# Encoder layer on one core: eight U blocks loaded during the query projection, four more at the start of the seam, seven gathers moved from the seam to the stage before it, and the loop's gathers spread by a table

## The chip, the cores and the metric

The kernel runs on one core of one Trainium2 chip. The metric is the device time of one execution in microseconds. Three runs of the kernel before took 1572.16, 1577.76 and 1579.21 us; the median, 1577.76 us, is what the new time is compared with.

## The reference

One transformer layer on 512 tokens of width 1024, all in float32. Two attentions and a projection come first; they matter here only as what runs before. The part that the change touches is the mixture of 16384 experts ("PEER") behind them:

```
q   = h @ w_q                          # 8 heads x 256, two halves of 128
s1, s2 = q1 @ keys0, q2 @ keys1        # 128 scores each; top 16 of each
idx = e1 * 128 + e2                    # top 16 of the 16x16 sums: 128 experts per token
hpre = sum_d x[t,d] * u_table[idx[t,e], d]
act  = softmax_weight * gelu(hpre)
out  = sum_e act[t,e] * v_table[idx[t,e], :]
h    = layer_norm(alpha*h + out + sigmoid(h @ gate_w + b) * (p @ ple_w))
```

U and V have 16384 rows of 1024 numbers (64 MB each).

## The kernel before, in words

The 512 tokens are four chunks of 128, and the experts of a token are found in one of two ways.

**Chunk 0 by gathers.** For each of its 128 slots k, GpSimd issues an indirect DMA that brings for all 128 tokens the row `u[idx[:,k]]` (128 rows of 4 KB, 0.524 MB), and VectorE multiplies it with h and sums it (`gather_u`, L1148; `rows`, L888). After all 128 and a Gelu, 128 more gathers bring V rows, and VectorE adds each, scaled, to the output (`gather_v`, L1157). That is 257 steps in all (128 U, one Gelu, 128 V).

**Chunk 1** has its U part done by gathers too (`own_rows`, 128 of them), its V part densely. **Chunks 2 and 3 (256 tokens, `N_U`) densely:** every block of 128 U rows (0.524 MB) is multiplied with the tokens on TensorE, and a Gelu follows. One-hot products turn the selected weights into a dense matrix G, which is stored in DRAM (`g_dram`); in the main loop G times the Gelu is split in a high and a low part and multiplied with the V block of 128 experts (three products for float32 accuracy).

In order of time:

1. **Query projection**, 16 groups (loop at L700): SP loads a slice of `w_q` (0.524 MB) into a `raw` buffer (three of them), ScalarE and VectorE cut it in two parts, TensorE multiplies. Then VectorE finds the top 16.
2. **Lead stage** (L1067 to L1097), written out by hand on all engines. TensorE works through 105 (`LEAD`) U blocks (`lead_block`, L935) that are mixed with the gate projection and the one-hot products; how many lie between two VectorE steps is set by a running account (`run_pe`, L812). `lead_block` keeps three loaded or loading blocks ahead in the `raw` buffers (`load_u`, L915). VectorE does the routing (`route`), the one-hot matrices (`build_g`, L821), and the products of the gathered rows. These come in the buffers `whi`, `wlo` and `row`, two of each. With the last `build_g`, chunk 0's first 24 (`BESIDE`) gathers run; then come the closing `pb.close()` and the next stage.
3. **The seam** (L1191 to L1210), also by hand: seven gathers are issued by GpSimd into `gat` buffers (eight, `GATS`), then GpSimd's two loads of the first G tile (`g_near`); the rest of the U blocks, the first three V blocks, and gathers up to step 42 (`PRE`), so that 18 gathers stand in the seam.
4. **Main loop** (L1214), 128 V blocks: in the first 23 passes (n from 0 to 22) one more U block is also loaded and multiplied by `expert_in` (L637) in three products. SP loads the V block and, from n = 28, a stored Gelu `ge`. G tiles are loaded some passes ahead (`g_loads`). In each pass some of the remaining 215 gather steps are run: the counter `spent` grows by 1 for n from 1 to 22, then by a half (`LATE`), and the steps done follow it. VectorE and SP run in the written order; a gather's product on VectorE stands behind the pass's own split.
5. Four layer norms and stores.

Each engine runs its instructions in order, so a wait holds all that is queued behind it. SP's DMAs are issued in order as well.

Of the kernel before, what the change touches and what calls it, by code (L numbers as in the profile page):

```python
# [9 lines left out]
F32 = mybir.dt.float32  # L10
# [26 lines left out]
WIDE = 40  # L37
LEAD = 105
# [4 lines left out]
LAG = 6.0  # L43
PRE = 42
BESIDE = 24
OWN = 1.2
OWN_G = 0.65
OWN_LATE = 10.0
LATE = 0.5
OT = 8  # L50
# [5 lines left out]
GATS = 8  # L56
NO_GATHER = 1
# [12 lines left out]
def tile_encoder_layer(ctx: ExitStack, tc: tile.TileContext, A: dict, out: bass.AP):  # L70
    nc = tc.nc
# [613 lines left out]
    def sub_scores(g, ps):  # L685
# [38 lines left out]
    pb = ExitStack()  # L724
    bt = pb.enter_context(tc.tile_pool(name="bt", bufs=2, side="right", reuse_waits="tile"))
    rg = pR.enter_context(tc.tile_pool(name="rg", bufs=1, reuse_waits="tile"))
# [183 lines left out]
    raws = []  # L910
# [3 lines left out]

    def load_u():  # L915
        nonlocal loaded
        if loaded < LEAD:
            raw = wst.tile([128, 8, 128], F32, name="raw", bufs=3)
            raws.append((loaded, raw))
            ins = nc.sync.dma_start(raw, A["uT"][loaded])  # L920
            if not loaded:
                tc.keep_in_program_order(ins)
            loaded += 1
# [11 lines left out]
    def lead_block():  # L935


        while len(raws) < 3 and loaded < LEAD:
            load_u()
        if not raws:  # L940
            return
        i, raw = raws.pop(0)
        ps = psH.tile([128, 512], F32, name="hp") if gating else ps_tile("mm", 4)
        for k in range(8):
            nc.tensor.matmul(ps[:, :N_U], raw[:, k], whole[:, k, :], start=(k == 0), stop=(k == 7))  # L945
            if k == 3 and last:
                leave_u(*last.pop())
            if k % 2 and tasks:
                tasks.pop(0)()
            yield PRODUCT_U  # L950
        last.append((i, ps))
# [115 lines left out]
    with tc.manual_schedule(engines={nc.vector.engine, nc.scalar.engine, nc.tensor.engine, nc.sync.engine,  # L1067
                                     nc.gpsimd.engine}):
        for _ in range(3):
            load_u()  # L1070
# [120 lines left out]
    with tc.manual_schedule(engines={nc.vector.engine, nc.scalar.engine, nc.tensor.engine, nc.sync.engine,  # L1191
                                     nc.gpsimd.engine}):
        gating = True
        some = [fetch_u(0, BESIDE + k) for k in range(GATS - 1)]
        for lo, hi in ((128 // GT, NTG), (0, 128 // GT)):
            load_g(0, lo, hi, nc.gpsimd)
        blocks_ahead(2)
        v_next = [load_v(n) for n in range(2)]
        for u in range(7):
            gather_u(0, BESIDE + u, some[u])  # L1200
# [3 lines left out]
        for n in range(2):  # L1204
            v_cut[n] = cut_v(n)
            blocks_ahead(1)
        for k in range(BESIDE + 7, PRE):
            gather_u(0, k)
        for _ in pe_work:
            pass  # L1210
    done, spent = PRE, 0
    with tc.manual_schedule(engines={nc.vector.engine, nc.sync.engine}):
        expert_in(LEAD)
        for n, i in enumerate(order):  # L1214
# [44 lines left out]
            for x in g_loads.get(n, []):  # L1259
                load_g(*x)  # L1260
            if n >= NO_GATHER:
                spent += 1 if n + LEAD < 128 else LATE
            upto = min(len(steps), PRE + math.ceil((len(steps) - PRE) * spent / (128 - (1 - LATE) * LEAD - 3 - NO_GATHER)))
            for f in steps[done:upto]:
# [107 lines left out]
```

## Time and profile before

| | before |
|---|---|
| median of three runs | 1577.76 us |
| profiled execution, its own time | 1580.15 us |
| its span, first to last instruction | 1578.2 us |
| mean granted TensorE clock | 0.988 |
| TensorE matmul busy | 1505.8 us (95%) |
| VectorE busy | 1298.2 us (82%) |
| DMA moved | 460.40 MB, mean 292 GB/s |

Times in the profile count from the span's start. A row of a timeline gives start, duration, engine, line, instruction, number merged, and in brackets how long the engine had been idle and what ended that. In a table of windows the columns are the busy time of each engine in that stretch (number of instructions in brackets), then the granted TensorE clock (1.00 is full speed), the mean busy share of the 16 DMA engines, and what they moved. A single matmul's record is longer than its place in the row of matmuls, since they are pipelined, so rows that merge many are used for durations.

### The profile page before, as it was taken

The numbers are of one execution on the slowest core, as the hardware profiler recorded it, in microseconds if no ns is written. First come the engines' busy times: TensorE is split into PE (matmuls) and PEld (weight loads), VectorE is DVE, ScalarE is ACT, GpSimd is POOL, SyncE is SP. The second block draws the span as 40 slices with busy tenths as digits, with TensorE's granted clock in tenths as the row PEclk, the third lists the DMA queues.
The fourth block names the chain that finished last, engine by engine and source line by source line (L and its number), as shares of the span: only waits on it lengthen the run. The fifth ranks groups of instructions, "written<-read, shape, count | busy, mean of one in ns | idle before, by whom it ended". The sixth has DMA issues, their size and how long they took to land.

```text
span 1578.2 us, 22819 instructions
## 1 busy us (share of the span) xinstructions
PE 1505.8 (95%) x7707; PEld 1267.9 (80%) x7707; DVE 1298.2 (82%) x3022; ACT 657.3 (42%) x1234; POOL 565.8 (36%) x521
## 2 busy tenths in 40 slices
PE   6999999999998999999999978999799999999997
PEld 4788777788887889789889967888588888788885
DVE  7376685679889799898889738998699899898997
ACT  3365675333222566167425512443233333333333
POOL 1023100020014334443323146555445666565630
PEclk9999999999999999999999999999999999999998
DMA  7242241142379899999989799999999999999972
GB/s 230 64 116 88 79 121 41 55 149 81 99 235 349 306 392 392 409 416 417 417 321 410 283 390 393 390 399 392 338 393 370 398 386 399 395 392 398 387 300 80
DMA packets 202532, 460.40 MB, mean 292 GB/s; under 512 B 17968, under 2 KB 104368, under 8 KB 199344
## 3 DMA queue, kind: packets, MB, share of 16 engines
q1 hardware_dynamic: 127888, 213.55, 38.1%
q0 software_dynamic: 58400, 208.69, 34.5%
q10 hardware_dynamic: 16128, 36.71, 6.0%
q8 instruction: 61, 1.00, 0.3%
q14 instruction: 55, 0.45, 0.1%
HBM read 415.11 MB, written 40.89 MB: 289 GB/s over the span
## 4 chain that ended last, share of the span: by engine, by line
PE 62%; DMA 19%; DVE 13%; issue 3%; ACT 2%; SPq 1%; POOL 0%; ACTq 0%; POOLq 0%; DVEq 0%
PE mm L945 7%; PE acc L108 6%; PE acc L109 6%; PE acc L110 6%; PE hp L945 6%; DMA raw<-in_v_rows_dram 6%; PE mm L108 4%; PE mm L110 4%; DMA v_raw<-in_v_rows_dram 4%; PE mm L109 4%; PE tr L841 4%; PE pj L108 3%; PE pj L109 3%; DMA raw<-in_uT_dram 3%; PE pj L110 3%
## 5 line engine op out<-in xcount | busy, mean ns | idle before, releaser
L1159 POOL DMA_INDIRECT gat<-in_v_rows_dram,i_sel x128 | 217.3, 1697 | 138.8 <-DVE base L1161 115.6
L945 PE MATMUL mm<-whole,raw 128*128 128x256 f32 x1088 | 244.0, 380 | 3.3 <-DMA raw<-in_uT_dram 3.0
L945 PEld LDWEIGHTS mm<-whole,raw 128*128 128x128 f32 x1088 | 202.5, 190 | 32.7 <-ACT ge L927 3.9
L108 PE MATMUL acc<-v_hi,a_hi 128*128 128x512 f32 x456 | 180.1, 397 | 15.8 <-ACT a_hi L93 15.6
L93 ACT CAST whi<-raw 128x1024 fp32r<-128x1024 f32 (+4 forms) x118 | 118.4, 1003 | 182.7 <-DMA raw<-in_v_rows_dram 60.4
L1144 POOL DMA_INDIRECT gat<-in_u_rows_dram,i_sel x104 | 136.0, 1308 | 147.9 <-DVE gat L1150 89.9
L110 PE MATMUL acc<-v_hi,a_lo 128*128 128x512 f32 x456 | 179.9, 396 | 0.1
L109 PE MATMUL acc<-v_lo,a_hi 128*128 128x512 f32 x456 | 179.3, 395 | 0.2 <-DVE v_lo L94 0.2
L94 DVE TENSOR_TENSOR wlo<-raw,whi 128x1024 fp32r<-128x1024 f32 (+4 forms) x118 | 136.7, 1159 | 40.8 <-ACT whi L93 39.9
L1161 DVE SCALAR_TENSOR_TENSOR base<-gat,hdot,base 128x1024 f32<-128x1024 f32 x128 | 163.8, 1280 | 1.5
L945 PE MATMUL hp<-whole,raw 128*128 128x256 f32 x592 | 137.1, 389 | 11.5 <-DMA raw<-in_uT_dram 11.0
L1150 DVE SCALAR_TENSOR_TENSOR gat<-gat,h 128x1024 f32<-128x1024 f32 x104 | 122.8, 1218 | 28.3 <-DMA gat<-in_u_rows_dram,i_sel 28.3
L93 ACT CAST v_hi<-v_raw 128x1024 fp32r<-128x1024 f32 x76 | 79.9, 1051 | 146.2 <-DMA v_raw<-in_v_rows_dram 123.3
L945 PEld LDWEIGHTS hp<-whole,raw 128*128 128x128 f32 x592 | 114.7, 195 | 29.6 <-issue 12.2
L892 POOL DMA_INDIRECT whi<-in_u_rows_dram,s_ix x43 | 45.9, 1069 | 208.3 <-DVE cand L745 132.5
L108 PE MATMUL acc<-whi,a_hi 128*128 128x512 f32 x300 | 117.2, 391 | 2.8 <-ACT a_hi L93 2.8
L110 PE MATMUL acc<-whi,a_lo 128*128 128x512 f32 x300 | 117.4, 391 | 0.0
L109 PE MATMUL acc<-wlo,a_hi 128*128 128x512 f32 x300 | 117.0, 390 | 0.0
L875 DVE TENSOR_SCALAR oh_j<-iota,eT 128x128 f32<-128x128 f32 x384 | 116.3, 375 | 0.0
L108 PEld LDWEIGHTS acc<-v_hi,a_hi 128*128 128x128 f32 x456 | 86.6, 191 | 36.1 <-ACT a_hi L93 18.9
L110 PEld LDWEIGHTS acc<-v_hi,a_lo 128*128 128x128 f32 x456 | 86.9, 190 | 21.1 <-DVE a_lo L94 2.9
L109 PEld LDWEIGHTS acc<-v_lo,a_hi 128*128 128x128 f32 x456 | 87.0, 191 | 18.6 <-DVE v_lo L94 0.9
(367 smaller groups left out, 3326.4 us busy)
## 6 DMA issues: line engine op xcount, KB each, us to landing
raw<-in_uT_dram SPq DMA_DIRECT2D x128, 512.0 KB
v_raw<-in_v_rows_dram SPq DMA_DIRECT2D x78, 512.0 KB
raw<-in_v_rows_dram SPq DMA_DIRECT2D x50, 512.0 KB
g_dram<-g_st ACTq DMA_DIRECT2D x24, 1024.0 KB
ge_dram<-ge ACTq DMA_DIRECT2D x88, 128.0 KB
ge<-ge_dram SPq DMA_DIRECT2D x88, 128.0 KB
g_wide<-g_dram SPq DMA_DIRECT2D x9, 1024.0 KB
raw<-in_w_in_dram SPq DMA_DIRECT2D x17, 512.0 KB
```

Of the source, the lines that this page charges most:

```text
L93: nc.scalar.copy(hi, src)
L94: nc.vector.tensor_tensor(lo, src, r32(hi), op=OP.subtract)
L108: nc.tensor.matmul(ps, a[0], b[0], start=start, stop=False)
L109: nc.tensor.matmul(ps, a[0], b[1], start=False, stop=False)
L110: nc.tensor.matmul(ps, a[1], b[0], start=False, stop=stop)
L841: nc.tensor.matmul(ps[:, i * 128:(i + 1) * 128], oj[:, 4 * r + i, :], oi[:, 4 * r + i, :], start=True, stop=True)
L875: nc.vector.tensor_scalar(oj[:, i], iota, eT[:, 1, t0 + i:t0 + i + 1], eT[:, 2, t0 + i:t0 + i + 1], op0=OP.is_equal, op1=OP.mult)
L945: nc.tensor.matmul(ps[:, :N_U], raw[:, k], whole[:, k, :], start=(k == 0), stop=(k == 7))
L1144: nc.gpsimd.indirect_dma_start(out=u[:], out_offset=None, in_=u_rows, in_offset=bass.IndirectOffsetOnAxis(ap=i_sel[:, c, k:k + 1], axis=0))
L1150: nc.vector.scalar_tensor_tensor(u, u, 1.0, h[c], op0=OP.mult, op1=OP.mult, accum_out=hdot[:, c, k:k + 1])
L1159: nc.gpsimd.indirect_dma_start(out=u[:], out_offset=None, in_=v_rows, in_offset=bass.IndirectOffsetOnAxis(ap=i_sel[:, c, k:k + 1], axis=0))
L1161: nc.vector.scalar_tensor_tensor(base[c], u, hdot[:, c, k:k + 1], base[c], op0=OP.mult, op1=OP.add)
```

## The change

- **Eight early blocks.** `EARLY` = 8: in the query projection's loop, groups 8 to 15 also allocate a buffer in a new pool (32 KB of each partition) and load one of the first eight U blocks into it. The pool lies where the one-hot buffers (`bt`) will be; these are now opened only at the first `build_g`, when the eight blocks are used up. `load_u` takes these eight as they are; `lead_block` counts only blocks in `raw` buffers, so three of those are still loaded ahead, and the first of them is block 8. On SP one of the eight loads stands ahead of the fifth `w_q` slice, three ahead of the sixth and four ahead of the eighth.
- **Four blocks at the seam's start.** The two `whi` and two `wlo` buffers, free once the gathered rows in them are used, take the next four U blocks beside the three in `raw`.
- **Gathers.** `BESIDE` goes from 24 to 31, `PRE` from 42 to 41: 31 of chunk 0's gathers now stand before the seam, ten in it (four of these, `SOME`, ahead of GpSimd's G loads, instead of seven).
- **Pace in the loop.** Each pass gets a share of the remaining 216 steps in proportion to `room(n)`: 2.6 up to n = 22, 0.9 up to 39, 1.35 up to 111, 1.9 up to 124.

Counted from the two formulas, steps done at the end of pass n:

| n | 0 | 22 | 39 | 111 | 121 | 124 |
|---|---|---|---|---|---|---|
| before | 42 | 109 | 134 | 242 | 257 | 257 |
| after | 41 | 105 | 122 | 230 | 251 | 257 |

```diff
-PRE = 42
-BESIDE = 24
+PRE = 41
+SOME = 4
+EARLY = 8
+BESIDE = 31
-LATE = 0.5
...
+    pU = ExitStack()
+    early = pU.enter_context(tc.tile_pool(name="early", bufs=1, side="right", reuse_waits="tile"))
+    early_u = []
     for g in range(16):
...
+        if g >= 16 - EARLY:
+            early_u.append(early.tile([128, 8, 128], F32, name=f"early{len(early_u)}"))
+            nc.sync.dma_start(early_u[-1], A["uT"][len(early_u) - 1])
         w = stream(A["w_q"][:, g * 128:(g + 1) * 128].rearrange("(k p) n -> p k n", p=128), [8, 128])
...
-    def load_u():
+    def load_u(name="raw"):
         nonlocal loaded
         if loaded < LEAD:
-            raw = wst.tile([128, 8, 128], F32, name="raw", bufs=3)
-            raws.append((loaded, raw))
-            ins = nc.sync.dma_start(raw, A["uT"][loaded])
...
+            if loaded < EARLY:
+                raw = early_u[loaded]
+            else:
+                raw = wst.tile([128, 8, 128], F32, name=name, bufs=3 if name == "raw" else 2)
+                ins = nc.sync.dma_start(raw, A["uT"][loaded])
...
+            raws.append((loaded, raw, loaded >= EARLY and name == "raw"))
...
-        while len(raws) < 3 and loaded < LEAD:
+        while sum(x[2] for x in raws) < 3 and loaded < LEAD:
...
-        some = [fetch_u(0, BESIDE + k) for k in range(GATS - 1)]
+        for name in ("whi", "whi", "wlo", "wlo"):
+            load_u(name)
+        some = [fetch_u(0, BESIDE + k) for k in range(SOME)]
...
-        for u in range(7):
+        for u in range(SOME):
             gather_u(0, BESIDE + u, some[u])
...
-        for k in range(BESIDE + 7, PRE):
+        for k in range(BESIDE + SOME, PRE):
...
+    def room(n):
+        if n < NO_GATHER or n > 124:
+            return 0.0
+        return 2.6 if n + LEAD < 128 else 0.9 if n < WIDE else 1.35 if n < 112 else 1.9
+
+    rooms = sum(room(n) for n in range(128))
...
-            if n >= NO_GATHER:
-                spent += 1 if n + LEAD < 128 else LATE
-            upto = min(len(steps), PRE + math.ceil((len(steps) - PRE) * spent / (128 - (1 - LATE) * LEAD - 3 - NO_GATHER)))
+            spent += room(n)
+            upto = min(len(steps), PRE + math.ceil((len(steps) - PRE) * spent / rooms))
```

Line numbers in the rows that follow are one to fourteen higher after than before. GpSimd's order before, from the last gather that goes with `build_g` to the main loop (`gat` rows are gathers of chunk 0):

```order
L892 DMA whi<-in_u_rows_dram,i_sel 128x1024
L892 DMA wlo<-in_u_rows_dram,i_sel 128x1024
L892 DMA row<-in_u_rows_dram,i_sel 128x1024
L1144 DMA gat<-in_u_rows_dram,i_sel 128x1024 x7
L1118 DMA g_near<-g_dram 128x16x128
L1118 DMA g_near<-g_dram 128x8x128
L1144 DMA gat<-in_u_rows_dram,i_sel 128x1024 x97
```

And after, where seven more `whi`, `wlo` and `row` gathers stand ahead of this piece:

```order
L899 DMA wlo<-in_u_rows_dram,i_sel 128x1024
L899 DMA row<-in_u_rows_dram,i_sel 128x1024
L899 DMA whi<-in_u_rows_dram,i_sel 128x1024
L1158 DMA gat<-in_u_rows_dram,i_sel 128x1024 x4
L1132 DMA g_near<-g_dram 128x16x128
L1132 DMA g_near<-g_dram 128x8x128
L1158 DMA gat<-in_u_rows_dram,i_sel 128x1024 x93
```

The G loads stand behind four `gat` gathers instead of seven, and behind 31 earlier ones instead of 24.

SP's order at the same place, before (the rows at L101 are the loop's own U blocks):

```order
L920 DMA raw<-in_uT_dram 128x1024 x73
L1134 DMA v_raw<-in_v_rows_dram 128x1024 x2
L920 DMA raw<-in_uT_dram 128x1024 x2
L1134 DMA v_raw<-in_v_rows_dram 128x1024
L920 DMA raw<-in_uT_dram 128x1024 x3
L101 DMA raw<-in_uT_dram 128x1024 x4
```

After:

```order
L929 DMA raw<-in_uT_dram 128x1024 x72
L929 DMA whi<-in_uT_dram 128x1024 x2
L929 DMA raw<-in_uT_dram 128x1024
L929 DMA wlo<-in_uT_dram 128x1024 x2
L929 DMA raw<-in_uT_dram 128x1024
L1148 DMA v_raw<-in_v_rows_dram 128x1024 x3
L102 DMA raw<-in_uT_dram 128x1024 x4
```

All six remaining lead blocks now go ahead of the three V blocks, and the loop's first U block is the tenth load from the first `whi`.

ScalarE's order from the last store of G to the loop's first split, before (`ge<-hp` frees one of two accumulators of a U block, `whi<-raw` cuts the loop's first U blocks, `v_hi` a V block):

```order
L854 DMA g_dram<-g_st 128x2048
L927 ACTIVATE ge<-hp 128x256 x3
L93 CAST v_hi<-v_raw 128x1024
L927 ACTIVATE ge<-hp 128x256
L93 CAST v_hi<-v_raw 128x1024
L927 ACTIVATE ge<-hp 128x256 x3
L93 CAST whi<-raw 128x1024
L927 ACTIVATE ge<-hp 128x256
L93 CAST whi<-raw 128x1024
L927 ACTIVATE ge<-hp 128x256
L93 CAST a_hi<-g_near 128x384
```

After:

```order
L861 DMA g_dram<-g_st 128x2048
L937 ACTIVATE ge<-mm 128x256 x2
L937 ACTIVATE ge<-hp 128x256 x3
L94 CAST v_hi<-v_raw 128x1024
L94 CAST whi<-raw 128x1024
L937 ACTIVATE ge<-hp 128x256
L94 CAST v_hi<-v_raw 128x1024
L94 CAST whi<-raw 128x1024
L937 ACTIVATE ge<-hp 128x256 x3
L94 CAST a_hi<-g_near 128x384
```

The first cut of a loop U block (`whi<-raw`) has come forward: four Gelus of lead blocks stand behind it now, and two before.

More of the change, by code (lines that the diff above doesn't have):

```diff
@@ L724, in tile_encoder_layer @@
     pb = ExitStack()
-    bt = pb.enter_context(tc.tile_pool(name="bt", bufs=2, side="right", reuse_waits="tile"))
+    bt = None
     rg = pR.enter_context(tc.tile_pool(name="rg", bufs=1, reuse_waits="tile"))
@@ L913, in tile_encoder_layer @@
     loaded = 0
-    def load_u():
+    def load_u(name="raw"):
         nonlocal loaded
         if loaded < LEAD:
-            raw = wst.tile([128, 8, 128], F32, name="raw", bufs=3)
-            raws.append((loaded, raw))
-            ins = nc.sync.dma_start(raw, A["uT"][loaded])
-            if not loaded:
-                tc.keep_in_program_order(ins)
+            if loaded < EARLY:
[3 more added lines that the diff above has]
+                ins = nc.sync.dma_start(raw, A["uT"][loaded])
+                if loaded == EARLY:
+                    tc.keep_in_program_order(ins)
+            raws.append((loaded, raw, loaded >= EARLY and name == "raw"))
             loaded += 1
@@ L941, in lead_block @@
             return
-        i, raw = raws.pop(0)
+        i, raw, _ = raws.pop(0)
         ps = psH.tile([128, 512], F32, name="hp") if gating else ps_tile("mm", 4)
@@ L1068, in tile_encoder_layer @@
                                      nc.gpsimd.engine}):
-        for _ in range(3):
+        for _ in range(EARLY + 3):
             load_u()
@@ L1078, in tile_encoder_layer @@
             run(route(c, res), OWN)
+            if bt is None:
+                assert all(x[0] >= EARLY for x in raws)
+                pU.close()
+                bt = pb.enter_context(tc.tile_pool(name="bt", bufs=2, side="right", reuse_waits="tile"))
             run(build_g(c, *res, OV_OWN), OWN)
```

## Prediction

> **What bounds the kernel now.** I read the page's slices first, then tables of windows, then TensorE's timeline where it idles.
>
> ```profile
> span 1578.2 us, 22819 instructions
> PE 1505.8 (95%) x7707; PEld 1267.9 (80%) x7707; DVE 1298.2 (82%) x3022; ACT 657.3 (42%) x1234; POOL 565.8 (36%) x521
> ...
> PE   6999999999998999999999978999799999999997
> ...
> PEclk9999999999999999999999999999999999999998
> DMA  7242241142379899999989799999999999999972
> ```
>
> TensorE is busy nearly everywhere, so only its gaps can be won. Slices are 39.5 us wide; the 7 and 8 behind twenty-three slices lie at 907 to 986, and the next 7 from 1105. DMA is at seven tenths or more from the 12th slice (434 us) almost to the end. The windows show both:
>
> ```profile
> 340.00:400.00 60.00, 60.00 (x300) 49.36 (x300) 57.75 (x314) 19.66 (x28) 0.00 (x0) 1.00 0.27 80
> 400.00:460.00 60.00, 60.00 (x286) 50.90 (x285) 52.24 (x269) 15.04 (x24) 0.00 (x0) 1.00 0.45 137
> 640.00:760.00 120.00, 119.72 (x656) 106.59 (x655) 106.38 (x264) 66.95 (x162) 52.43 (x49) 1.00 1.03 414
> 880.00:907.00 27.00, 27.00 (x165) 24.86 (x164) 17.33 (x48) 13.81 (x32) 2.52 (x3) 1.00 0.67 225
> 907.00:1160.00 253.00, 225.90 (x1204) 192.92 (x1204) 196.02 (x303) 80.60 (x118) 132.12 (x102) 0.97 1.02 384
> 1160.00:1520.00 360.00, 359.03 (x1573) 294.15 (x1572) 329.68 (x401) 131.59 (x176) 218.94 (x129) 1.00 1.03 392
> 1520.00:1560.00 40.00, 40.00 (x176) 32.41 (x175) 35.26 (x55) 15.43 (x22) 0.00 (x0) 1.00 0.36 128
> ```
>
> ```profile
> 900.00:1000.00 100.00, 84.13 (x425) 71.41 (x424) 58.73 (x92) 24.91 (x41) 51.47 (x42) 0.95 0.99 376
> 1000.00:1100.00 100.00, 100.00 (x607) 89.54 (x606) 93.21 (x142) 39.59 (x56) 58.65 (x44) 1.00 1.04 393
> 1100.00:1160.00 60.00, 48.77 (x218) 38.35 (x217) 44.09 (x70) 17.79 (x27) 24.52 (x19) 0.94 0.98 357
> ```
>
> From 907 on DMA is saturated (share 1.02, 1.03) until the gathers end; before that lies a hole (880 to 907: 0.67), and behind it another (1520 to 1560: 0.36). TensorE idles 15.9 us in 900 to 1000 and 11.2 in 1100 to 1160, and its clock there, 0.95 and 0.94, costs 5.0 and 3.6 us more. So 35.7 us can be won behind 900, and 1.0 us after 1160. What ends the gaps in the seam:
>
> ```profile
> 916.77 3.69 PE L945 MATMUL hp<-whole,raw 128*128 128x256 f32 x16 [2.87 <-DMA raw<-in_uT_dram]
> 924.56 8.83 PE L945 MATMUL hp<-whole,raw 128*128 128x256 f32 x32 [4.09 <-DMA raw<-in_uT_dram]
> ...
> 945.66 0.39 PE L108 MATMUL hp<-hTh,whi 128*128 128x256 f32 x1 [1.18 <-ACT ge L927]
> ...
> 950.48 0.50 PE L108 MATMUL acc<-v_hi,a_hi 128*128 128x512 f32 x1 [0.97 <-ACT a_hi L93]
> 970.30 1.65 PE L108 MATMUL acc<-v_hi,a_hi 128*128 128x512 f32 x3 [4.75 <-ACT a_hi L93]
> ```
>
> And between 1100 and 1160, of all engines' waits:
>
> ```profile
> ACT whi L93 <- DMA raw<-in_v_rows_dram: 15.3, 3, 7.2
> ...
> PE acc L108 <- ACT a_hi L93: 11.0, 4, 5.7
> ACT v_hi L93 <- DMA v_raw<-in_v_rows_dram: 10.9, 2, 8.8
> ```
>
> TensorE waits for ScalarE, and ScalarE for V blocks. In 1000 to 1100 TensorE never idles, yet the traffic asked for is over what DMA gives, and the V blocks fall behind until the buffers are empty at 1100. Both gaps are thus a debt of DMA, and a gather not issued before them pays it back. One gather is 0.524 MB, at the 384 GB/s of 907 to 1160 1.365 us.
>
> **Early blocks: nothing.** TensorE is busy 60.00 of 60 us in both windows from 340 to 460, and DMA has room (0.27 and 0.45). So eight loads less at the start of the lead stage free what nobody wants, and from block 8 on it still looks three blocks ahead. The wait inside it stays:
>
> ```profile
> 509.49 6.65 PE L945 MATMUL hp<-whole,raw 128*128 128x256 f32 x16 [4.08 <-DMA raw<-in_uT_dram]
> ...
> 518.78 3.61 PE L945 MATMUL hp<-whole,raw 128*128 128x256 f32 x16
> ```
>
> On SP the eight loads pass `w_q` slices, four of them in a row ahead of the eighth. Their cover is that low DMA share and the three `raw` buffers. Were it gone, it would cost at most 8 x 0.524 MB at 414 GB/s, 10.1 us, and 3.0 us of slow clock (6.65 against 3.61 above). I take 0; below nothing is excluded, since no TensorE idle time is there to be won.
>
> **Seven gathers into the hole.** GpSimd stood still there:
>
> ```profile
> 877.06 1.86 POOL L1144 DMA_INDIRECT gat<-in_u_rows_dram,i_sel  x1 [0.30 <-ACT oh_i L866]
> 903.87 0.94 POOL L1144 DMA_INDIRECT gat<-in_u_rows_dram,i_sel  x1 [24.96 <-ACT g_st L852]
> ```
>
> The `gat` buffers lie on the one-hot buffers; `whi`, `wlo` and `row` don't, so gathers 24 to 30 can go as those come free. The hole holds 27 us x (414 - 225) GB/s = 5.1 MB; seven gathers are 3.67 MB. Their products cost VectorE time:
>
> ```profile
> L894 DVE SCALAR_TENSOR_TENSOR wlo<-wlo,h 128x1024 f32<-128x1024 f32 x8 | 9.7, 1213 | 0.0
> ```
>
> Seven at 1.213 us are 8.5 us, two of them still inside `build_g`, five behind it (counted in the new order). Behind them wait the `gat` products and the loop's first split; in the seam VectorE is busy only 58.73 of 100 us, and the same seven no longer stand there. I price that at 0; if it were not covered it would be 2.4 us, the two inside.
>
> **The four U loads ahead** let TensorE have up to seven blocks loading instead of three. They end the waits of 2.87 and 4.09 us, but add no bandwidth; they are part of the seam's term.
>
> **The sum by stages.** Steps between the last gather of `build_g` and the end of a pass, from the table of steps: to n = 22, before 109 - 24 = 85, after 105 - 31 = 74, so 11 fewer; to n = 39, before 134 - 24 = 110, after 122 - 31 = 91, 19 fewer. Where n = 22 lies, this row of SP's tells:
>
> ```profile
> L101 SPq DMA_DIRECT2D raw<-in_uT_dram x23: 327/328/1857, 937.6 to 1095.1; - x23
> ```
>
> So the 11 fall into 907 to 1100, the other 8 mostly into 1100 to 1160.
>
> - *Seam:* 11 x 1.365 = 15.0 us less of DMA time, against 20.9 us of idle time and slow clock. The lower bound is 7.5: the lead blocks' products behind the last one-hot product (68 in the new order), each 2 x 3.61 / 16 us, are 30.7 us of TensorE work from 903, so the loop's first U block comes at 934 to 938 instead of 945.66, and `acc` at about 943. Not all the debt turns into time, since the first G tile and the gathers still have to land one after another. I take 12.
> - *Gap at 1100:* 8 x 1.365 = 10.9 us, against 14.8. From 0 (the debt falls due later) to 14.8. I take 10.9, since the wait there is for V blocks alone.
> - *Passes 40 to 111:* both 108 steps; TensorE is busy 359.03 of 360 us. 0.
> - *Passes 112 to 124:* 27 steps instead of 15 by 121. VectorE's rows there:
>
> ```profile
> L1161 DVE SCALAR_TENSOR_TENSOR base<-gat,hdot,base 128x1024 f32<-128x1024 f32 x121 | 154.9, 1280 | 1.5
> L94 DVE TENSOR_TENSOR wlo<-raw,whi 128x1024 fp32r<-128x1024 f32 x44 | 53.6, 1219 | 0.0
> ...
> L94 DVE TENSOR_TENSOR a_lo<-g_wide,a_hi 128x384 fp32r<-128x384 f32 x45 | 24.9, 553 | 15.3 <-ACT a_hi L93 15.2
> ...
> L1244 DVE TENSOR_TENSOR g_wide<-g_wide,ge 128x256 f32<-128x256 f32 x46 | 19.2, 417 | 0.0
> ```
>
> From 1160 to 1520, 1573 matmuls at 18 a pass are 87.4 passes of 4.12 us, of which VectorE is busy 3.77. With 27/13 = 2.08 gathers a pass instead of 1.5 it has 0.58 x 1.28 = 0.74 us more: 4.51. Thirteen passes fall 13 x 0.39 = 5.1 us behind. VectorE is ahead by a pass, since its splits have two buffers each, and that covers 4.1. DMA has 27 + 13 blocks and some Gelus, 21.5 MB, at 392 GB/s 54.8 us for passes that take 53.6. So from 0 to 5.1; I take 2.
>
> Sum: -12 - 10.9 + 2 = -20.9. The profiled execution took 1580.15 us, which gives 1559.2; it lies 2.4 us over the median of the runs, so against 1577.76 the forecast is **1557 us**.
>
> On the clock: behind the wait of 4.08 us 16 matmuls took 6.65 us, behind that of 2.87 us 3.69. [...]
>
> **Rivals.**
>
> *A, DMA takes it back (0.20).* If DMA bounds everything from 907 to the last gather, only the 3.67 MB moved in front count: 3.67 / 0.384 = 9.6 us, and 1568. For it: share 1.03 for 360 us on end. Against it: 0.36 in 1520 to 1560, where the twelve late gathers find room. [...]
>
> *B, slower: the loop's first U block lands late (0.05).* It is SP's tenth load from the first `whi`, which itself waits for VectorE's product of gather 27. ScalarE now cuts it ahead of four Gelus, each of which frees an accumulator, so TensorE stops after two more blocks. Before:
>
> ```profile
> 944.28 1.04 ACT L93 CAST whi<-raw 128x1024 fp32r<-128x1024 f32 x1 [6.29 <-DMA raw<-in_uT_dram]
> ```
>
> Ten loads are 5.24 MB. With half of 384 GB/s they land by 931, ahead of need; with a quarter by 958. `acc` would then start at about 963, 12.7 us late instead of early, and 3.0 us of slow clock come on top: 15.7 - 10.9 + 2 = +6.8, or 1585. From a landing after 955 nothing is won. Against it: in the seam before, SP's U blocks did not starve to a quarter, as the row shows (issued at 937.6, there at 944.28).
>
> *C, the early loads hold up `w_q` (0.05):* 20.9 - 13.1 leaves 7.8, or 1570.
>
> *D, all gaps close (0.08):* 35.7 us, 1542.
>
> **How the numbers follow.** The forecast has 0.60, and 0.02 is left for what I don't see. About 0.5% (7.9 us) is what a measurement of this kernel can tell from no change. Faster by more: 0.60, D's 0.08, two thirds of A, half of C: 0.84. Within: the rest of A and C: 0.10. Slower: B and the unseen: 0.06. The forecast's own bounds run from 7.5 + 5.5 - 5.1 = 7.9 us (half the gap's term) to 15.0 + 14.8 = 29.8; A on one side and a part of D on the other make the range 1544 to 1571.
>
> **What would show it.** Right: DMA above 350 GB/s in the 27 us up to the last one-hot product; the first `acc` 6 to 9 us earlier; no waits of TensorE for U blocks in the seam, none over 2 us around the last loop U block; gathers until about 25 us before TensorE's end; the wait at 505 unchanged. Wrong: idle time of TensorE between 340 and 420 (C), ScalarE waiting for the first loop U block over 15 us (B), a new gap of TensorE between passes 60 and 111 (A), or waits for `a_lo` or `v_lo` of more than 5 us in the last thirteen passes.

## The result

Five runs of the changed kernel took 1563.62 to 1570.05 us, median 1566.07, against 1577.76 for the kernel before on the same chip: a ratio of 0.993 (95% interval 0.9906 to 0.9953), 11.7 us faster. The profiled execution took 1565.61 us. The page of the changed kernel:

```profile
span 1563.8 us, 22811 instructions
PE 1499.1 (96%) x7707; PEld 1268.0 (81%) x7707; DVE 1300.4 (83%) x3022; ACT 657.4 (42%) x1234; POOL 554.6 (35%) x521
...
PE   6999899999998999999999979999999999999996
...
PEclk9999999999999999999999999999999999999998
DMA  7242341182239899999989999999999999999992
```

One weak slice is left in the seam (the 7), the one at 1105 is gone, and the last slice has fallen from 7 to 6. The same windows as before the change:

```profile
340.00:400.00 60.00, 60.00 (x296) 49.20 (x296) 57.73 (x315) 19.22 (x28) 0.00 (x0) 1.00 0.31 90
400.00:460.00 60.00, 60.00 (x286) 50.99 (x285) 52.16 (x270) 15.75 (x26) 1.02 (x1) 1.00 0.21 69
880.00:907.00 27.00, 27.00 (x169) 24.96 (x168) 25.38 (x60) 14.50 (x33) 7.58 (x9) 1.00 0.97 368
900.00:1000.00 100.00, 91.19 (x487) 80.13 (x486) 65.42 (x103) 29.72 (x47) 48.31 (x38) 0.95 1.01 380
1000.00:1100.00 100.00, 100.00 (x602) 89.36 (x601) 92.27 (x140) 39.14 (x56) 56.15 (x42) 1.00 1.04 393
1100.00:1160.00 60.00, 56.73 (x254) 46.77 (x253) 46.93 (x75) 21.20 (x29) 19.75 (x18) 0.97 1.05 381
1160.00:1520.00 360.00, 358.83 (x1574) 294.26 (x1573) 331.14 (x403) 130.97 (x175) 214.79 (x131) 1.00 1.02 385
1520.00:1560.00 40.00, 28.78 (x122) 22.15 (x120) 38.50 (x79) 12.99 (x21) 0.00 (x0) 0.90 0.32 118
```

The hole ahead of the seam is filled (368 GB/s instead of 225), TensorE idles 8.8 us in 900 to 1000 instead of 15.9, and 3.3 in 1100 to 1160 instead of 11.2. What TensorE waits for in the seam and at the gap:

```profile
917.78 5.24 PE L955 MATMUL hp<-whole,raw 128*128 128x256 f32 x16 [2.96 <-DMA raw<-in_uT_dram]
...
939.22 6.45 PE L955 MATMUL hp<-whole,wlo 128*128 128x256 f32 x16 [5.84 <-ACT ge L937]
...
951.81 0.39 PE L109 MATMUL acc<-v_hi,a_hi 128*128 128x512 f32 x1
...
1121.48 0.50 PE L109 MATMUL acc<-whi,a_hi 128*128 128x512 f32 x1 [3.27 <-ACT a_hi L94]
```

One wait for a U block stays, and a wait of 5.84 us for a Gelu is new. The first `acc` comes at 951.81, not at about 943: 1.3 us later than before. ScalarE's rows tell why:

```profile
930.15 1.04 ACT L94 CAST v_hi<-v_raw 128x1024 fp32r<-128x1024 f32 x1 [3.26 <-DMA v_raw<-in_v_rows_dram]
937.84 1.04 ACT L94 CAST whi<-raw 128x1024 fp32r<-128x1024 f32 x1 [6.65 <-DMA raw<-in_uT_dram]
938.79 0.38 ACT L937 ACTIVATE ge<-hp 128x256 f32<-128x256 f32 x1
```

It stood 6.65 us at the cut of the loop's first U block, with the Gelu that frees TensorE's accumulator behind it. That is rival B's order in a mild form (15 us of waiting were named as its sign).

Executions scatter by several microseconds, and a stage's start moves with all that lies ahead of it. So the trace is cut into stages, each measured from its own start. The table holds all profiles of this study. Lead: from the first one-hot product's start to the last one's end. Then from there to the first `acc` product of pass 6; pass 6 to 21; 21 to 30 (the gap at 1100 lies there); 30 to 112; 112 to the last `acc` product; from that product's start to the end of the span. Passes are counted off in TensorE's timeline, 18 `acc` products each; every profile has all 2304 of them.

| kernel | lead | to 6 | 6 to 21 | 21 to 30 | 30 to 112 | 112 to last | end |
|---|---|---|---|---|---|---|---|
| before | 374.6 | 99.4 | 105.3 | 56.0 | 338.3 | 65.5 | 10.7 |
| changed | 378.3 | 87.6 | 105.0 | 45.0 | 337.4 | 67.5 | 15.2 |
| changed, second profile | 377.1 | 87.4 | 105.0 | 47.6 | 336.7 | 67.8 | 15.2 |
| early blocks alone | 375.9 | 101.1 | 105.8 | 53.5 | 337.8 | 65.5 | 10.7 |
| pace alone | 378.4 | 98.4 | 106.5 | 45.5 | 335.5 | 67.5 | 15.1 |
| old pace | 379.1 | 88.2 | 106.6 | 54.5 | 338.1 | 65.5 | 10.8 |
| pace to 121 | 376.5 | 86.9 | 105.0 | 46.3 | 346.1 | 67.3 | 11.5 |
| no early blocks | 377.8 | 88.0 | 105.0 | 46.7 | 338.7 | 69.8 | 15.2 |
| no four blocks | 379.8 | 87.7 | 105.0 | 40.6 | 339.5 | 69.4 | 15.2 |
| late cut | 377.1 | 83.8 | 105.0 | 45.3 | 338.0 | 68.2 | 15.2 |
| late cut 2 | 381.6 | 88.1 | 105.0 | 42.3 | 340.3 | 67.5 | 15.2 |
| norm off VectorE | 377.2 | 87.1 | 104.7 | 46.6 | 340.6 | 67.5 | 16.1 |
| late cut 2, norm off | 377.1 | 85.8 | 104.7 | 45.4 | 339.5 | 68.1 | 16.1 |
| no four, norm off | 377.8 | 89.6 | 104.7 | 41.4 | 338.4 | 68.1 | 16.1 |

Read down the columns. The seam with ten gathers instead of 18 gives 12 us up to pass 6; the new pace gives 8 to 11 from pass 21 to 30; and the new pace takes back 2.0 and 2.3 behind pass 112 and 4.5 behind the last product. The last loss is the one that the prediction has no term for. The norm of chunk 0 on VectorE, before:

```profile
1536.21 1.28 DVE L1161 SCALAR_TENSOR_TENSOR base<-gat,hdot,base 128x1024 f32<-128x1024 f32 x1
...
1538.88 1.28 DVE L126 BATCH_NORM_STATS2 ln_st<-base 128x6 f32<-128x512 f32 x2
...
1548.04 1.28 DVE L149 SCALAR_TENSOR_TENSOR base<-base,ln_y,gat 128x1024 f32<-128x1024 f32 x1
...
1567.58 0.39 PE L110 MATMUL acc<-v_hi,a_lo 128*128 128x512 f32 x1
...
1572.68 1.28 DVE L149 SCALAR_TENSOR_TENSOR h<-h,ln_y,gat 128x1024 f32<-128x1024 f32 x1
```

And after:

```profile
1532.89 2.60 DVE L1175 SCALAR_TENSOR_TENSOR base<-gat,hdot,base 128x1024 f32<-128x1024 f32 x2
...
1540.76 0.55 DVE L95 TENSOR_TENSOR a_lo<-g_near,a_hi 128x384 fp32r<-128x384 f32 x1
1541.23 1.28 DVE L127 BATCH_NORM_STATS2 ln_st<-base 128x6 f32<-128x512 f32 x2
...
1548.62 0.39 PE L111 MATMUL acc<-v_hi,a_lo 128*128 128x512 f32 x1
...
1549.35 1.29 DVE L150 SCALAR_TENSOR_TENSOR base<-base,ln_y,gat 128x1024 f32<-128x1024 f32 x1
...
1558.13 1.28 DVE L150 SCALAR_TENSOR_TENSOR h<-h,ln_y,gat 128x1024 f32<-128x1024 f32 x1
```

The first row of each is the last gather's product, the rows with `ln_st<-base` and `base<-base,ln_y` are the start and the end of chunk 0's norm, the row of `acc` is TensorE's last product, and the last row is VectorE's last instruction. Chunk 0 can be normalised only when its last gather is added. Before, that was at 1537.5, and the norm ran between the splits of the last passes; it was done 18 us ahead of the last `acc`. Now the last gather's product ends at 1535.5 and belongs to pass 124; behind it stand the splits of the last three passes (the `a_lo` at 1540.76 is the last), and VectorE does the norm behind them all, in among the norms of the other three chunks. It is done 2.0 us behind the start of the last `acc`.

### The profile page after: what moved, and what is told of

Same layout as the page of the kernel before. It is cut to its first block, busy times and chain, and to the rows that moved or that the text cites. A ratio compares the mean times of both kernels' runs of the same rounds, so it can differ in the third digit from the quotient of the medians.

```text
span 1563.8 us, 22811 instructions
## 1 busy us (share of the span) xinstructions
PE 1499.1 (96%) x7707; PEld 1268.0 (81%) x7707; DVE 1300.4 (83%) x3022; ACT 657.4 (42%) x1234; POOL 554.6 (35%) x521
## 4 chain that ended last, share of the span: by engine, by line
PE 61%; DMA 18%; DVE 15%; issue 3%; ACT 2%; SPq 1%; POOL 0%; ACTq 0%; DVEq 0%
PE mm L955 9%; DMA raw<-in_uT_dram 7%; PE acc L109 6%; PE acc L111 6%; PE acc L110 6%; PE hp L955 5%; PE tr L848 5%; DMA raw<-in_v_rows_dram 4%; PE mm L109 4%; PE mm L111 3%; PE mm L110 3%; PE pj L109 3%; PE pj L110 3%; PE pj L111 3%; DMA v_raw<-in_v_rows_dram 3%
## 5 line engine op out<-in xcount | busy, mean ns | idle before, releaser
L1173 POOL DMA_INDIRECT gat<-in_v_rows_dram,i_sel x128 | 211.9, 1656 | 136.3 <-DVE base L1175 105.5
L955 PE MATMUL mm<-whole,raw 128*128 128x256 f32 x1120 | 251.1, 380 | 5.9 <-DMA raw<-in_uT_dram 5.1
L955 PEld LDWEIGHTS mm<-whole,raw 128*128 128x128 f32 x1120 | 209.0, 190 | 36.0 <-ACT ge L937 5.1
L109 PE MATMUL acc<-v_hi,a_hi 128*128 128x512 f32 x456 | 176.9, 390 | 0.3 <-ACT a_hi L94 0.2
L1158 POOL DMA_INDIRECT gat<-in_u_rows_dram,i_sel x97 | 125.2, 1290 | 139.7 <-DVE gat L1164 108.6
L94 ACT CAST v_hi<-v_raw 128x1024 fp32r<-128x1024 f32 x76 | 79.8, 1051 | 106.3 <-DMA v_raw<-in_v_rows_dram 87.7
L1164 DVE SCALAR_TENSOR_TENSOR gat<-gat,h 128x1024 f32<-128x1024 f32 x97 | 114.8, 1221 | 10.9 <-DMA gat<-in_u_rows_dram,i_sel 10.9
L95 DVE TENSOR_TENSOR v_lo<-v_raw,v_hi 128x1024 fp32r<-128x1024 f32 x76 | 93.3, 1227 | 26.3 <-ACT v_hi L94 26.3
L110 PEld LDWEIGHTS acc<-v_lo,a_hi 128*128 128x128 f32 x456 | 85.6, 188 | 17.6 <-DVE v_lo L95 0.2
L848 PEld LDWEIGHTS tr<-oh_i,oh_j 128*128 128x128 f32 x768 | 93.7, 192 | 4.5 <-ACT g_st L859 1.1
## 6 DMA issues: line engine op xcount, KB each, us to landing
ge<-ge_dram SPq DMA_DIRECT2D x88, 128.0 KB, 12.5
```

The costliest lines, as they stand in the source:

```text
L94: nc.scalar.copy(hi, src)
L95: nc.vector.tensor_tensor(lo, src, r32(hi), op=OP.subtract)
L109: nc.tensor.matmul(ps, a[0], b[0], start=start, stop=False)
L110: nc.tensor.matmul(ps, a[0], b[1], start=False, stop=False)
L848: nc.tensor.matmul(ps[:, i * 128:(i + 1) * 128], oj[:, 4 * r + i, :], oi[:, 4 * r + i, :], start=True, stop=True)
L1158: nc.gpsimd.indirect_dma_start(out=u[:], out_offset=None, in_=u_rows, in_offset=bass.IndirectOffsetOnAxis(ap=i_sel[:, c, k:k + 1], axis=0))
```

## The experiments

Each kernel was timed against the kernel before on the same chip. Kernels that shared a chip share the median of before in the table, and medians are compared among these.

| kernel | median, us | before, us | ratio, 95% interval |
|---|---|---|---|
| early blocks alone | 1580.56 | 1579.18 | 1.0007, 0.9990 to 1.0024 |
| pace alone | 1572.06 | 1579.18 | 0.9957, 0.9942 to 0.9971 |
| old pace | 1568.66 | 1579.18 | 0.9935, 0.9921 to 0.9948 |
| pace to 121 | 1567.99 | 1579.18 | 0.9934, 0.9914 to 0.9954 |
| changed, again | 1564.21 | 1578.51 | 0.9916, 0.9891 to 0.9941 |
| no early blocks | 1567.74 | 1578.51 | 0.9917, 0.9896 to 0.9938 |
| no four blocks | 1562.42 | 1578.51 | 0.9888, 0.9866 to 0.9911 |
| late cut | 1560.15 | 1578.51 | 0.9890, 0.9868 to 0.9912 |
| norm off VectorE | 1565.21 | 1581.33 | 0.9903, 0.9881 to 0.9925 |
| late cut 2 | 1564.58 | 1581.33 | 0.9897, 0.9875 to 0.9919 |
| late cut 2, norm off | 1564.12 | 1581.33 | 0.9899, 0.9872 to 0.9925 |
| no four, norm off | 1563.66 | 1581.33 | 0.9897, 0.9870 to 0.9924 |

**Early blocks alone.** The edit is the pool `early` with its eight loads and what `load_u` needs to take them; all else is as before:

```diff
+EARLY = 8
...
+        if g >= 16 - EARLY:
+            early_u.append(early.tile([128, 8, 128], F32, name=f"early{len(early_u)}"))
+            nc.sync.dma_start(early_u[-1], A["uT"][len(early_u) - 1])
...
```

> The kernel before with the eight early U blocks as its only change: the seam with its 18 gathers, BESIDE, PRE and the old pace stay. Theory (the early blocks give nothing, since TensorE idled nowhere between 340 and 460): 0 against the kernel before, within 2 us, about 1578; the two gaps at 907 to 986 and at 1100 to 1140 stay as they were. Rival E (the early blocks carry a good part of the 11.7 us that the whole change gained): 5 us faster or more. Rival C (they hold up the projection's own slices): 8 to 13 us slower, with idle time of TensorE between 340 and 420.

Measured 1.0007: nothing, as the theory said. The two windows that it changes have TensorE as full as ever:

```profile
340.00:400.00 60.00, 60.00 (x296) 49.19 (x296) 57.74 (x315) 19.08 (x27) 0.00 (x0) 1.00 0.31 90
400.00:460.00 60.00, 60.00 (x286) 50.99 (x285) 52.15 (x268) 15.95 (x26) 1.25 (x2) 1.00 0.20 67
```

**No early blocks**, the same part undone in the changed kernel:

```diff
-EARLY = 8
+EARLY = 0
```

> The changed kernel without early blocks: all lead blocks are loaded by the lead stage as before, the rest stays. Theory (the early blocks give nothing, alone or beside the rest): within 2 us of the changed kernel; first one-hot product where it was, about 526 to 528. Rival E (alone they were hidden, but here they give DMA to the seven gathers in the hole): 3 to 6 us slower than the changed kernel, and DMA from 820 to 907 fuller than its 385 GB/s with waits for U blocks in it.

The ratio is 0.9917 beside 0.9916 for the changed kernel on the same chip. The median is 3.5 us longer, which would fit rival E, but the intervals don't tell the two apart. The first one-hot product starts at 526.46. DMA moves 393 GB/s from 820 to 907, over the 385 that rival E named, but TensorE waits for no U block there, and the stages show no cost: lead 377.8, to pass 6 88.0. The early blocks do nothing alone and nothing that shows beside the rest.

**Pace alone**, the kernel before with the new table:

```diff
+    def room(n):
+        if n < NO_GATHER or n > 124:
+            return 0.0
+        return 2.6 if n + LEAD < 128 else 0.9 if n < WIDE else 1.35 if n < 112 else 1.9
...
-            if n >= NO_GATHER:
-                spent += 1 if n + LEAD < 128 else LATE
+            spent += room(n)
...
```

> The kernel before with the new pace of the loop's gathers alone: 18 gathers in the seam, no early blocks, no U blocks in the gather buffers. Up to pass 39 it issues 11 gathers fewer than the kernel before, 3 of them up to pass 22. Theory (a gather not issued ahead of the gap at 1100 pays it back): 11 x 1.365 = 15.0 us less of DMA time, of which the gap takes 10.9 to 14.8; the seam stays; the last passes lose 2.0 and the norm of chunk 0 behind the last matmul 3.8. Together 5 to 9 us faster than before, about 1571. Rival A (DMA is the bound from the seam to the last gather, so an order of gathers wins nothing): no gain in the gap that lasts, and 2.0 + 3.8 on top, 1 slower to 6 slower. Rival I (the gap closes only when the seam's gathers are fewer too): half of it, 0 within 2 us.

Measured 7.1 us, inside 5 to 9. This answers rival A: no gather was moved in front of the seam, none was dropped, and yet the gap shrank for good. The window 1100 to 1160:

```profile
1100.00:1160.00 60.00, 56.26 (x263) 46.76 (x262) 45.02 (x70) 20.83 (x30) 18.32 (x17) 0.97 1.04 378
```

The idle time is 3.7 us there instead of 11.2. From 21 to 30 it gains 10.5, and it pays 2.0 behind pass 112 and 4.4 at the end.

**Old pace**, the changed kernel with the formula of before in place of `room`:

```diff
-            spent += room(n)
+            if n >= NO_GATHER:
+                spent += 1 if n + LEAD < 128 else LATE
...
```

> The changed kernel with the old pace of the loop's gathers: early blocks, the seven gathers in the hole and the four U blocks stay. Theory (the two halves add up): the seam's 8.8 us and no more, about 1569 in the median, since the gap at 1100 comes back (passes 6 to 24 keep the lead of 9 us, and pass 30 has lost none of it and won nothing); the last instruction of VectorE lies again 6 to 7 us behind the last matmul, since the gathers end at pass 121. Rival I (the two halves need each other): 0 to 4 us faster than before alone. Rival E2 (the seam's gain comes from the pace, which issues three gathers less by pass 22): less than 5 us faster than before.

Measured 10.5 us, the theory's 8.8 or a little more. The gap is back, and the end is at 10.8 us:

```profile
1100.00:1160.00 60.00, 51.52 (x217) 40.09 (x216) 44.83 (x73) 18.91 (x27) 24.10 (x19) 0.91 1.00 358
```

From the last one-hot product to pass 30 the kernel before takes 260.7 us, pace alone 250.4, the seam's part alone 249.3; if the gains add up, both together give 239.0, and the changed kernel's two profiles have 237.6 and 240.0. In this stretch the halves add up. The seam's half holds three things: the gathers moved ahead of it, the early blocks and the four U blocks. The other experiments find nothing for either kind of U block, which leaves the gathers; no run has the moved gathers alone.

**Changed, again**, unaltered:

> The changed kernel once more, unaltered, on the chip of the three kernels that follow, since the profiles of two kernels with the same seam began that seam up to 5 us apart. If the two halves add up as their own medians say (10.5 us for the seam's part with the old pace, 7.1 for the pace), it lies 17 us under the kernel before, 1562. If they overlap, 11 to 13 us under it, 1567. From the last one-hot product's end to the first matmul of pass 6 it takes 86 to 89 us in either case (before: 99.4), since that stretch is the seam without the scatter ahead of it.

14.3 us under the kernel before, after 11.7 in the first timing; 17.6 would be the sum of the two halves' medians. Each of these has an uncertainty of 2 to 4 us, so the overlap is not settled by the times; by the stages there is none up to pass 30. The seam is 87.4 us again.

**Pace to 121**, the gathers ended three passes earlier, six more of them in passes 40 to 111:

```diff
-        if n < NO_GATHER or n > 124:
+        if n < NO_GATHER or n > 121:
             return 0.0
-        return 2.6 if n + LEAD < 128 else 0.9 if n < WIDE else 1.35 if n < 112 else 1.9
+        return 2.6 if n + LEAD < 128 else 0.9 if n < WIDE else 1.43 if n < 112 else 1.9
```

> The changed kernel with the gathers ended at pass 121 instead of 124: the pace is 1.43 instead of 1.35 in passes 40 to 111, which then have 114 gathers instead of 108, and 1.9 from 112 to 121. Theory (the 3.8 us behind the last matmul are chunk 0's norm, which needs the last gather's product and had lain beside passes 124 to 127): 3 to 5 us faster than the changed kernel, VectorE's last instruction 6 to 7.5 us behind the last matmul, 1562. Rival T (the tail is longer because VectorE is late with everything by then, whatever it does last): no change within 1.5 us. Rival A (passes 40 to 111 have no room left in DMA, share 1.03): the six gathers more cost up to 8.2 us there, and the kernel is 0 to 4 us slower than the changed one.

Both the theory and rival A hold, each in its place. The end is 11.5 us instead of 15.2: chunk 0's norm is among the splits again. And passes 30 to 112 take 346.1 instead of 337.4 and 336.7, about 9 us for six gathers at 1.365 us (8.2). The window 1300 to 1420, of the changed kernel:

```profile
1300.00:1420.00 120.00, 119.75 (x525) 97.78 (x524) 110.08 (x132) 42.48 (x57) 76.62 (x44) 1.00 1.04 391
```

and with the pace to 121:

```profile
1300.00:1420.00 120.00, 115.40 (x484) 91.84 (x483) 106.37 (x126) 40.22 (x55) 72.24 (x44) 0.97 1.04 391
```

At the same 391 GB/s TensorE now idles 4.6 us and loses 3.6 to the clock. So these passes have room for the 108 gathers that both kernels gave them, and not for 114. The two effects cancel: 0.9934, as the kernel with the old pace on the same chip and as the changed kernel in its first timing (0.993).

**No four blocks.** The lines that load the next U blocks into the `whi` and `wlo` buffers are left out:

```diff
-        for name in ("whi", "whi", "wlo", "wlo"):
-            load_u(name)
```

> The changed kernel without the four U blocks in the gather buffers: the lead stage looks three blocks ahead to its end, and the gathers, the early blocks and the pace stay. Theory (they let TensorE have its blocks in time): the waits of 2.9 and 4.1 us for U blocks behind 907 come back, with up to 3 us of slow clock, 3 to 8 us slower than the changed kernel. Rival A (they add no bandwidth, so they only displace gathers and V blocks): within 2 us. Rival B (they push the loop's first U block back, for which ScalarE and then TensorE waits): that wait of 5.84 us goes instead, 2 to 5 us faster.

The theory falls. Waits for U blocks come back in the seam, 0.74, 0.66 and 4.45 us, but of the 5.84 for a Gelu only 2.65 are left, and it is as far at pass 6 (87.7) and 4 to 7 us ahead at pass 30. In time it is 1.8 us ahead of the changed kernel, which is not told apart. What the four blocks did is seen in DMA's rate from 907 to 960, of the changed kernel:

```profile
907.00:960.00 53.00, 44.20 (x205) 37.94 (x204) 23.76 (x39) 11.72 (x20) 26.24 (x21) 0.90 0.99 365
```

and without the four:

```profile
907.00:960.00 53.00, 44.03 (x207) 37.41 (x206) 22.43 (x34) 11.69 (x20) 20.34 (x19) 0.94 1.02 380
```

15 GB/s over 53 us are 0.8 MB, one and a half gathers or 2.1 us of DMA time. The gap goes the way of such a debt: pass 21 to 30 takes 45.0 and 47.6 us with the four blocks, 40.6 and (below) 41.4 without. But that is twice the 2.1 us and more, so the cause of this difference is not shown.

**Late cut.** The loop's first `expert_in` moves to the end of the seam's block, so that ScalarE cuts its U block behind the last Gelus:

```diff
         for _ in pe_work:
             pass
+        expert_in(LEAD)
...
     with tc.manual_schedule(engines={nc.vector.engine, nc.sync.engine}):
-        expert_in(LEAD)
```

> The changed kernel with the loop's first expert_in moved to the end of the seam's block, so that ScalarE cuts the loop's first U block behind all the Gelus of lead blocks instead of ahead of four of them; the loads stay in their order. Theory (rival B in a mild form: the 5.84 us for which TensorE waited for ge at 939 was ScalarE standing at that cut, whose U block landed at 937.8): no such wait, TensorE goes from the last lead block straight to the products of pass 0; from the last one-hot product's end to pass 6 it takes 4 to 9 us less than the 87.6 of the changed kernel, and the kernel is 3 to 8 us faster. Rival D1 (the seam is bound by what DMA has to bring, whoever waits for it): the idle time moves to the next product, for the U block or for G, and the kernel is within 2 us of the changed one.

The wait of 5.84 us is gone, so its cause was that order. ScalarE and TensorE:

```profile
934.41 0.39 ACT L937 ACTIVATE ge<-hp 128x256 f32<-128x256 f32 x1 [3.07 <-PE hp L955]
934.69 1.99 ACT L94 CAST whi<-raw 128x1024 fp32r<-128x1024 f32 x2
```

```profile
930.76 3.62 PE L955 MATMUL hp<-whole,raw 128*128 128x256 f32 x16
934.02 0.58 PE L109 MATMUL acc<-v_hi,a_hi 128*128 128x512 f32 x1
...
939.99 0.39 PE L111 MATMUL hp<-hTh,wlo 128*128 128x256 f32 x1 [2.77 <-DVE wlo L95]
```

The first `acc` comes 33.8 us behind the last one-hot product instead of 45.6, about 3 of it because the loop's first U block now follows it. By pass 6 there are 3.7 left of the 11.8: a new wait of 2.77 us for VectorE, and the passes' own waits. So rival D1 takes a part, and the theory's 4 to 9 us are just missed in the stage. The time is 4.1 us under the changed kernel on the same chip, with intervals that overlap.

**Late cut 2**: the same, and VectorE makes `wlo` of that block ahead of the last six gather products:

```diff
         for _ in pe_work:
             pass
+        expert_in(LEAD)
         for k in range(BESIDE + SOME, PRE):
             gather_u(0, k)
```

> As the kernel with the late cut, but the loop's first expert_in stands ahead of the seam's last six gather products, so that VectorE makes wlo of the first loop U block before them (there TensorE waited 2.77 us for wlo at 939.99). Theory (the order of VectorE and ScalarE sets the seam): from the last one-hot product's end to pass 6 it takes 80 to 83 us, against 83.8 with the late cut and 87.4 to 87.6 in the changed kernel, and the kernel is 0 to 3 us faster than with the late cut, 1558 to 1561. Rival D1 (DMA's debt decides by pass 6): 83 to 85 us, no faster than with the late cut. Rival F (the six products set when the gather buffers come free): the gathers of the first passes are issued later, and it comes out 1 to 3 us slower than with the late cut.

The theory falls, and so does rival D1's 83 to 85 us: it takes 88.1 us to pass 6, with a wait of 3.04 for the same `wlo` and one of 3.8 for a U block. Its 1564.58 us were timed on another chip than the late cut, so rival F is not settled; the ratios are 0.9897 and 0.9890. From pass 21 to 30 it gains (42.3). To pass 30 it takes 235.4 us and the late cut 234.1, so between these two it is the place of the idle time that changed, and not its sum. What exactly sets pass 6 in this kernel was not found.

**Norm off VectorE.** Chunk 0's two 128x1024 products go to ScalarE and GpSimd:

```diff
+        if off:
+            nb = small.tile([128, 1], F32, name="ln_nb")
+            nc.vector.tensor_tensor(nb, mu[:, 0:1], y, op=OP.mult)
+            nc.vector.tensor_scalar(nb, nb, -1.0, None, op0=OP.mult)
+            nc.scalar.activation(r, r, AF.Identity, bias=nb, scale=y)
+            nc.gpsimd.tensor_tensor(r, r, g, op=OP.mult)
+            nc.gpsimd.tensor_tensor(r, r, b, op=OP.add)
+            return
...
```

> The changed kernel with the two 128x1024 products at the end of chunk 0's norm taken off VectorE (2 x 1.28 us): ScalarE does the scaling, GpSimd the factor and the summand, and GpSimd's queue stores the chunk. Theory (VectorE's order behind the last matmul is the end, and chunk 0's norm is what lengthened it): the last instruction of VectorE comes 2.0 to 3.5 us earlier against the last matmul than in the changed kernel, from 15.2 us between the last matmul's start and the end of the span to 11.7 to 13.2, and the time falls by as much. Rival S (the end is the chain of the last chunk through ScalarE and the store, and VectorE has room): within 1 us. Rival G (GpSimd's two products and their store become the last work): the span ends with GpSimd's store, 0 to 4 us later.

The end is 16.1 us, 0.9 longer, and VectorE's last instruction ends 12.5 us behind the start of the last product instead of 10.8: later, not 2.0 to 3.5 us earlier. GpSimd's two products, and VectorE beside them:

```profile
1546.95 3.06 POOL L151 TENSOR_TENSOR base<-base,gat 128x1024 f32<-128x1024 f32 x1 [29.42 <-ACT ln_sd L140]
1550.09 2.35 POOL L152 TENSOR_TENSOR base<-base,gat 128x1024 f32<-128x1024 f32 x1
```

```profile
1548.46 1.65 DVE L115 TENSOR_TENSOR ln_t<-ln_ve,ln_y 128x1 f32<-128x1 f32 x2
1550.02 0.15 DVE L133 TENSOR_TENSOR ln_mu<-fsum 128x1 f32<-128x1 f32 x1
1550.09 2.37 DVE L116 TENSOR_TENSOR ln_t<-ln_t,ln_y 128x1 f32<-128x1 f32 x2
1552.38 0.14 DVE L134 TENSOR_SCALAR ln_mu<-ln_mu 128x1 f32<-128x1 f32 x1
```

VectorE's products of 128x1, which take 0.16 us elsewhere, end when GpSimd's do: 1.65 and 2.37 us for two each. Neither the theory nor its rivals had that, and the rows don't show why the ends fall together. The four took 4.02 us instead of 0.64, 3.38 longer, which is over the 2.56 us (2 x 1.28) that VectorE was spared. So the saving went into these four, and the run leaves open what the end would be if VectorE were spared the two products without GpSimd.

**Late cut 2 with the norm off VectorE**, both edits:

> Both edits, the second late cut and the norm off VectorE. Theory (they lie 550 us apart and add up): 4 to 6 us for the cut and 2 to 3.5 for the norm, 6 to 9 us under the changed kernel, 1556 to 1559, under 0.988 of the kernel before. If the end of the span does not follow VectorE or the seam's gain is given back in the gap at 1120, 1560 or more.

0.9899, and 1564.12 us where 1556 to 1559 was expected: no better than either, as the two fell singly.

**No four blocks with the norm off VectorE:**

> The changed kernel without the four U blocks in the gather buffers and with chunk 0's norm off VectorE: a second look at the four blocks, whose removal gave 1562.4 against 1564.2, not told apart. Theory F0 (the four blocks are worth nothing): as the norm's edit alone, within 1.5 us. Theory F1 (they cost what their removal showed): 1.5 to 4 us under the norm's edit alone, with a gap of less than 43 us from pass 21 to pass 30 as in the removal's profile (40.6, against 45.0 and 47.6 in the two profiles of the changed kernel).

41.4 us from pass 21 to 30, as F1 said, but 89.6 to pass 6, and in time 1.5 us under the norm's edit alone, not told apart. Without the four blocks the last one-hot product to pass 30 takes 233.3 and 235.7 us, with them 237.6 and 240.0. No gain from the four blocks shows anywhere, and the stages speak for a cost of about 4 us that the times do not confirm. No kernel here is shown to beat the changed one; the late cut has the lowest median.

## Why the prediction was right, and where it was not

- *The mechanism*, a debt of DMA that a gather not issued pays back, is right: the pace alone closes the gap. The kernel was predicted at 1557 us and took 1566.07, inside the range. But the gain is 11.7 us in the first timing and 14.3 in the second, where 20.9 was forecast, and the first is nearer to rival A's 1568 than to 1557. The time alone could not have ruled A out; the pace alone and the stages do.
- *Early blocks, 0:* right, alone and beside the rest. The wait at 505 stayed (4.89 us).
- *Seam, -12:* right in size (99.4 to 87.6 and 87.4), wrong in place, so the size is in part luck. Of the 11.8 us only 1.8 are there at the first `acc`; the other 10 come in passes 0 to 5, where before a wait of 4.75 us lay and then 6.83 us at a granted clock of 0.50 (969.45 to 976.28). "`acc` at about 943" failed because ScalarE's order brought back what the four U loads were to save: TensorE waited for a Gelu instead of a U block. The late cut shows that it was this order, and rival B had named it. B's ten loads were issued from 903.8 on and the last was there at 937.8: 5.24 MB in 34 us, 154 GB/s, between the half of 384 at which B expected no cost and the quarter at which it expected `acc` 12.7 us late.
- *The four U loads "end the waits of 2.87 and 4.09 us":* they did not; 2.96 stayed, 5.84 came, and without the loads the seam is as long.
- *Gap at 1100, -10.9:* 11.0 and 8.4 in the two profiles. A wait of 3.27 us was left, where none over 2 was named. Without the four blocks it is 0.3.
- *Passes 40 to 111, 0:* right, and the pace to 121 shows how near the edge it was.
- *Passes 112 to 124, +2:* 2.0 and 2.3 up to the last product (up to 4.3 in the other kernels with this pace). VectorE limits them, as said: it is busy 66.5 of 67.5 us, before 57.2 of 65.5.
- *Seven gathers in the hole, 0:* the lead stage is 376.3 us in the mean of the three profiles with 24 gathers beside it (374.6 to 378.4), and 378.1 in the eleven with 31 (376.5 to 381.6). That is 1.8 us, near the 2.4 named for the case that the two products inside are not covered; the scatter of single profiles is as large.
- *The failed step* is a term that is missing. "Passes 112 to 124" costed the twelve late gathers in those passes alone, and not what waits for the last of them: chunk 0's norm. It left the cover of the last passes and cost 4.5 us behind the last product (10.7 to 15.2). In all four profiles whose gathers end at pass 121 the end is 10.7 to 11.5 us; in the ten with 124 it is 15.1 to 16.1.

In the sum, the first profile against before: -0.6 ahead of the lead stage, +3.7 lead, -11.8, -0.3, -11.0, -0.9, +2.0, +4.5 are -14.4, which is what the spans differ by. The three terms of the prediction's sum come to -20.8 of it, as forecast; what is missing is the 4.5 at the end and the 3.7 of the lead stage, whose profiles scatter by as much. Rival A was wrong as a whole (pace alone), though its mechanism is what binds passes 40 to 111. Of C no run shows a sign.

## What to carry to other kernels

When work is moved later, price not only the stage that it enters but also who waits for its last piece: here a norm that had been free lost its cover. Loading a block earlier won nothing here: the first eight because TensorE waited for no block where they helped, the four in the seam because ScalarE's order put a later arrival ahead of the Gelu for which TensorE waited. And when executions differ by more than the effect, measure each stage from its own start; the seam took 86.9 to 88.2 us in the six profiles that have the same seam, though it began anywhere from 899.7 to 907.1.

## What the hardware did that was not expected

The clock fell after shorter waits than the prediction's two rows had shown. In the kernel with the pace alone a wait of 1.95 us is followed by 16 products in 5.38 us instead of 3.62:

```profile
912.42 5.38 PE L944 MATMUL hp<-whole,raw 128*128 128x256 f32 x16 [1.95 <-DMA raw<-in_uT_dram]
```

With the old pace, a wait of 3.07 us at the same place cost nothing:

```profile
918.77 3.72 PE L956 MATMUL hp<-whole,raw 128*128 128x256 f32 x16 [3.07 <-DMA raw<-in_uT_dram]
```

So in these runs the length of one wait does not tell whether the clock falls. The traces of the kernel before and of the changed kernel show where it changes: in both, each stretch of granted clock between the first and the last lasts a whole multiple of 3.41 us (from 1 to 125 times), so the changes lie on a grid. On such a grid, the kernel with the pace alone:

```profile
909.98:913.39 3.41, 1.46 (x8) 0.99 (x7) 1.23 (x2) 0.38 (x1) 2.38 (x3) 1.00 1.02 418
913.39:916.80 3.41, 3.41 (x10) 2.70 (x9) 1.23 (x2) 1.04 (x1) 2.04 (x2) 0.50 1.03 418
```

and with the old pace:

```profile
913.75:917.16 3.41, 1.95 (x10) 1.37 (x8) 0.00 (x0) 0.38 (x1) 0.56 (x2) 1.00 0.95 362
917.16:920.57 3.41, 1.80 (x8) 1.62 (x9) 1.42 (x3) 0.00 (x0) 2.80 (x3) 1.00 1.03 414
920.57:923.98 3.41, 3.41 (x17) 3.00 (x17) 2.00 (x3) 0.38 (x1) 2.56 (x3) 1.00 1.03 368
```

The wait of 1.95 us falls into one slot of the grid, in which TensorE is busy for only 1.46 of 3.41 us, and the next slot has half the clock. The longer wait of 3.07 us is cut by an edge, both slots are busy for more than half, and the clock stays. In the traces of the kernel before and of the changed one, between 60 and 1530 us, half the clock follows on all 10 slots at full clock that were busy for less than 43%, on none of 834 busy for more than 49%, and on one of the two between. So what a wait cost here depended on where it fell, and the grid lay elsewhere in each execution: the clock halves at 925.08 us before, at 917.47 in the changed kernel and at 913.39 with the pace alone, 7.61 and 4.08 us apart, which are no whole multiples of 3.41.
